# Branch A's attention values in plain fp32 passes, two heads as column tiles of one matmul group

## The chip, the cores and the metric

The kernel runs on one core of one Trainium2 chip. The metric is the device time of one launch in microseconds (us). Lower is better.

## The reference

One encoder layer is applied to two request groups ("prompt" and "sample", each 1024 tokens by 1024 channels) that share all weights. What matters of it:

```python
h = rms_norm(x, norm_g) * (1.0 + scale) + shift          # scale, shift, gate from silu(c) @ w_ada
qa, ka, va, za, qb, kb, vb, zb, ga, gb = split(h @ w_in)  # one input projection

# Branch A: 8 query heads, 2 key/value heads, head_dim 64, QK RMSNorm, axial rotary
p  = softmax(qa @ ka.T / 8)              # per query head; four query heads share one k and one v
oa = (p @ va) * silu(za)
# Branch B: 4 heads with two 64-dim softmax maps each, 128-dim values
ob = rms_norm((p0 - lam * p1) @ vb) * (1 - lam_init) * silu(zb)

merged = sigmoid(ga) * (oa @ w_proj_a) + sigmoid(gb) * (ob @ w_proj_b)
y = x + gate * (merged @ w_out)
```

All inputs and outputs are fp32.

## The kernel before, in words

The two groups are worked one after the other. In each, the kernel makes the normalised and modulated input `h`, projects it, runs the attention of Branch A (phases 0 and 1, four query heads each) and of Branch B (phases 2 to 5, one head each), then the gates, the two branch projections, their merge and the output projection.

**Precision.** Most matmuls multiply a high and a low part: an fp32 value is cut by ScalarE into an fp32r part (`hi`) and by VectorE into the remainder (`lo`), and hi·hi, hi·lo and lo·hi are added in PSUM, each product one fast fp32r pass. A matmul on operands that are viewed as plain fp32 needs no such split and is run by TensorE in several passes of its own; the profile shows it as two records.

**Units of attention.** `units_of` makes a list of units, `attention` steps through them. In Branch A a unit is one query head and a pair of 128-query tiles (`pr`), 32 units for each group. `scores` handles one tile per step: the scores by two matmul passes for each half of the 1024 keys (lines 834 and 835, into one of two score banks `s`), the row maximum on VectorE (836), its scaling (837) and the exponential (838) on ScalarE, which writes a probability buffer `p` of `ppool` (four of them). `swapped` gets the queries with their halves exchanged by four small DMAs per two heads (688, tile `sw`). One step later `flip` transposes the probabilities in 32x32 blocks on VectorE (871) and carries them by four DMAs (876) into the unit's transposed tile `q` of `qpool` (two of them), where the blocks land so that keys lie on partitions.

`a_values` then multiplies with v. `pT_pieces` cuts each quarter of the transposed probabilities into `hi` (ScalarE, 884) and `lo` (VectorE, 885, in place in `q`). The weights are v's tile of 128 keys, 64 columns of its high part beside 64 columns of its low part; the moving operand is 256 queries, once `hi` (896) and once `lo` (897), for eight key chunks: 16 matmuls. `PV_LAG` keeps the matmuls two pieces behind the cutting. At the end one half of the accumulator is copied by ScalarE (912), the other half added by VectorE (913), and 64 rows go out by DMA (917). The halves of v's tile are written in `kva_gen` (711 and 712). Branch B's `b_values` (936), by `WHOLE`, already takes v and probabilities as plain fp32, with 128-column weights.

**Order of work.** Beside the attention run "pieces" of other work that TensorE can do meanwhile: input projections (598, with the transposes 658), gate projections in `z_gen` (807, results through `zd` in DRAM), branch projections (1080) and the output projection (1111). `weave` takes steps from several generators in proportion to weights and with head starts that are written out as constants at the top (`Z_SHARE`, `ATT_W`, `IN_A`, `Z_A`, `LAST_ATT` and others; one row for each request group, one entry for each phase). Attention steps are issued with a raised priority (`AHEAD`), and a scheduler that simulates a timeline settles the order on each engine; the chip then runs each engine's queue in order.

**Column tiles** occur in two places: the adaLN matmuls of the first group (`ada`, reported at line 104, four tiles of 32 columns) and those of the gate (`gate_gen`, 530, four tiles of which two columns are used).

**The start.** The first group's input arrives in quarters of channels; squares, sum, inverse root (307 to 314), the spreading of the norm over partitions (`spread`, 321), then `ada` on the first weights, `ada_sum`, and the modulation.

Of the kernel before, what the change touches and what calls it, by code (L numbers as in the profile page):

```python
# [12 lines left out]
F32 = mybir.dt.float32  # L13
F32R = mybir.dt.float32r
# [6 lines left out]
P = 128  # L21
# [14 lines left out]

Z_SHARE = (
    (8, 21, 4, 2, 4, 3),
    (13, 12, 7, 3, 0, 6),
)  # L40
Z_HEAD = (8, 6)
Z_HEAD_A = (-0.3, -0.32)
ATT_W = (
    (0.944, 1.067, 1.232, 1.093, 1.03, 1.769),
    (1.017, 1.367, 1.063, 1.196, 0.764, 1.069),
)
IN_A = (
    (0.1, -0.07, 0.7, 0.05, 0.25, 0.15),
    (0.1, -0.05, 0.43, 0.3, 0.15, 0.55),
)  # L50
Z_A = (
    (0.25, 0.05, 0.2, -0.05, -0.1, 0.0),
    (0.03, 0.05, 0.35, 0.15, -0.3, -0.2),
)
LAST_ATT = (47, 43)
LAST_FILL = (22, 23)
GATED_A = (0.1, 0.1)
LATE_A = 1.0
QUARTER_P = 200
KV_STEPS = 12  # L60
GATE_AT = 9
FIRST_ATT = 15
FIRST_A = 0.16
TAIL = (2, 5)
TAIL_A = (1.15, 1.15)
LAG = 2
Z_FIRST = (9, 8)
Z_FIRST_A = (-0.05, 0.0)

CUTS = (3, 6)  # L70

BEHIND = 1.4
AHEAD = 100
PV_LAG = 2

WHOLE = (True, True)

# [30 lines left out]
def kernel(ctx: ExitStack, tc: tile.TileContext, t: dict):  # L108
# [4 lines left out]
    upool = ent(tc.tile_pool(name="upool", bufs=15))  # L113
    wpool = ent(tc.tile_pool(name="wpool", bufs=2))
    spool = ent(tc.tile_pool(name="spool", bufs=3))
    ppool = ent(tc.tile_pool(name="ppool", bufs=4))
    qpool = ent(tc.tile_pool(name="qpool", bufs=2))
    tpool = ent(tc.tile_pool(name="tpool", bufs=2))
    mpool = ent(tc.tile_pool(name="mpool", bufs=2))
# [19 lines left out]
    def gbank():  # L139
        turn[0] += 1  # L140
        if alone[0] and not early and turn[0] % 5 in (0, 2):
            return sbank()[:, :512]
        return fbank()
# [179 lines left out]
        nc.scalar.activation(rsb, bank, AF.Copy)  # L323
        return rsb

    def ada(wts, cpad):

        acc = gbank()
        for q, wt in enumerate(wts):
            for c in range(4):  # L330
                pe.matmul(
                    acc[32 * c : 32 * c + 32], cpad[:, q * 4 + c], wt[:, c], start=(q == 0), stop=(q == 1),
                    tile_position=(0, 32 * c),
                )
        part = rtile()
        act.activation(part, acc, AF.Copy)
        return part

    def ada_sum(part):
        ps = gbank()[:, :8].rearrange("p (t c g) -> p t c g", t=2, g=2)  # L340
# [55 lines left out]
    def start(ht):  # L396
        cpad = mtile("at", [P, 256], bufs=1).rearrange("p (c m) -> p c m", c=NCH)
        nc.vector.memset(cpad, 0.0)
        nc.scalar.activation(cT, ccol, AF.Tanh, scale=0.5)
        nc.vector.scalar_tensor_tensor(out=cT, in0=cT, scalar=1.0, in1=ccol, op0=ALU.add, op1=ALU.mult)  # L400
        nc.vector.tensor_scalar(out=cT, in0=cT, scalar1=0.5, scalar2=None, op0=ALU.mult)
        nc.vector.tensor_copy(cpad[:, :, :2], cT)
        xT = [load_xT0(0)]
        dma_next(bcol, t["b_col"])
        dma_next(gcol, t["g_col"])
        wts = [load_ada(n) for n in range(2)]
        kva_w.append(load_w(w_cols(w_in, (C_KA, 256)), early=True))
        kva_w.append(load_w(w_cols(w_in, (C_QA, 256)), early=True))
        wts += [load_ada(n) for n in range(2, 8)]

        rs = inv_rms(added(squares(xT[0])))
        nc.vector.tensor_scalar(out=bcol[:, 1, :], in0=bcol[:, 1, :], scalar1=1.0, scalar2=None, op0=ALU.add)
        rsb = spread(rs)
        early.update({n: four_sums() for n in range(2)})
        ps = ada_sum(ada(wts[:2], cpad))
        with tc.high_priority(offset=QUARTER_P):
            for quarter in range(4):
                cs = range(quarter * 2, quarter * 2 + 2)
                by_rms(xT[0], cs, rsb)
                split_early(kva_w[0][1], quarter)  # L420
                ada_end(quarter, ps)
                if quarter % 2 == 0:
                    add_h(ht, 0, quarter // 2)
                split_early(kva_w[1][1], quarter, act)
                modulated(ht, 0, xT[0], cs)
                split_early(kva_w[1][1], quarter, vec)
                for c in cs:
                    sums_early(ht, c, 0)
                part = ada(wts[quarter * 2 + 2 : quarter * 2 + 4], cpad) if quarter < 3 else None
                for c in cs:  # L430
                    sums_early(ht, c, 1)
                    if part is not None:
                        ps, part = ada_sum(part), None
        xT.append(load_xT0(1))
        kva_w.append((load_w(w_cols(w_in, (C_ZA, 256)), room=(utile(), utile())),))
        return lambda: inv_rms(added(squares(xT[1]))), lambda rs: start_late(ht, xT[1], rs)
# [226 lines left out]
    def pipelined(ht, w, front, back, given={}, rest=0):  # L663
# [14 lines left out]
            back(*pend.pop(0))  # L678
        yield 1

    def swapped(u):

        qs = u["q"]
        sw = mtile("sw", [P, 2, 256], F32R)[:, : len(qs)]
        sl = slice(u["pr"] * 256, u["pr"] * 256 + 256)
        for m, q in enumerate(qs):
            for a, b in ((LO, HI), (HI, LO)):
                dma(sw[a, m].bitcast(F32), q[b, sl].bitcast(F32))
        return sw
# [7 lines left out]
    def kva_gen(ht, out):  # L697
        w = kva_w[0][0] if early else load_w(w_cols(w_in, (C_KA, 256)))
        given = dict(enumerate(early.get(0, ())))
        k = v2(utile())  # L700
        va = utile().rearrange("p (n k d) -> p n k d", n=NTT, k=2)
        out["ka"], out["va"] = k, va

        def front(tt, ps):
            e = by_turns(tt)
            rs = tiny.tile([P, 4], F32, tag="rs", name=nm("rs"))[:, :2]
            x3, s3 = rows(ps[:, :128], 2, rs)
            e.tensor_tensor(out=x3, in0=x3, in1=rs.unsqueeze(2).to_broadcast([P, 2, HD]), op=ALU.mult)
            vp = ps[:, 128:256].rearrange("p (k d) -> p k d", k=2)
            vt = va[:, tt]  # L710
            nc.scalar.activation(vt[:, :, 0:64], vp, AF.Copy)
            nc.vector.tensor_tensor(out=vt[:, :, 64:128], in0=vp, in1=vt[:, :, 0:64].bitcast(F32), op=ALU.subtract)
            e.tensor_tensor(out=x3, in0=x3, in1=gka.unsqueeze(1).to_broadcast([P, 2, HD]), op=ALU.mult)
            rope(x3, s3, out["cosA"][:, tt : tt + 1], out["sinA"][:, tt : tt + 1], 16, e)
            return x3
# [126 lines left out]

    def scores(u, i):

        nm_ = len(u["q"])
        t, m = i // nm_, i % nm_
        qt = u["pr"] * 2 + t
        if "sw" not in u:
            u["sw"] = swapped(u)
        pt = ptile()  # L850
        su = u["su"][:, qt : qt + 1] if m == 0 else tiny.tile([P, 1], F32, tag="su", name=nm("su"))
        softmax_unit(u["q"][m][:, qt * P : (qt + 1) * P], u["rs"](qt, m), u["sw"][:, m, t * P : (t + 1) * P], u["k"][m], pt, su)
        if m == 0:
            u[t] = [pt]
        else:
# [3 lines left out]
                out=f, in0=f, scalar1=u["su"][:, qt : qt + 1], scalar2=nlam, op0=ALU.mult, op1=ALU.mult  # L859
            )  # L860
            u[t] += [pt, f]
        return t if m == nm_ - 1 else None

    def flip(u, t):

# [20 lines left out]
            yield cc, th, tl  # L886

    def a_values(u):
        acc = ps_a.tile([P, 512], F32, tag="a", name=nm("a"))[:, :256]
        ready = []  # L890

        def pv(cc, th, tl):
            for c in range(2):
                k = cc * 2 + c
                lt = u["v"](k)
                nc.tensor.matmul(acc, lt, th[:, c, :], start=(k == 0), stop=False)  # L896
                nc.tensor.matmul(acc, lt, tl[:, c, :], start=False, stop=(k == 7))  # L897

        for piece in pT_pieces(u):
            ready.append(piece)  # L900
            if len(ready) > PV_LAG:
                pv(*ready.pop(0))
            yield 1
        while len(ready) > 1:
            pv(*ready.pop(0))
            yield 1
        pv(*ready.pop())
        tmp = mtile("at", [P, 256], bufs=1)
        o = mtile("oo", [P, 256])
        j = u["j"]  # L910
        a, b = (slice(0, 64), slice(64, 128)) if j % 2 == 0 else (slice(64, 128), slice(0, 64))
        nc.scalar.activation(tmp[a], acc[b], AF.Copy)
        nc.vector.tensor_tensor(
            out=query_order(o[a]), in0=piece_order(acc[a]), in1=piece_order(tmp[a]), op=ALU.add
        )
        pr = u["pr"]
        dma(u["od"][pr // 2][a, (pr % 2) * 256 : (pr % 2 + 1) * 256], o[a])
        yield 1

    def b_values(u):  # L920
# [238 lines left out]

    def units_of(st):  # L1160

        def a_unit(half, i, pr):
            j = half * 4 + i
            kv = j // 4
            return {
                "q": [st["qa"][half][i % 2][:, i // 2]], "k": [st["ka"][:, kv]],
                "v": (lambda k: st["va"][:, k, kv, :]),
                "pr": pr, "j": j, "od": st["od"][j // 2], "su": st["suA"][:, j],
                "rs": lambda qt, m: st["rsA"][:, half, qt, i : i + 1],
            }  # L1170

        def b_unit(h, pr):
# [11 lines left out]
        units = []  # L1184
        for half in range(2):
            units += [
                (half, lambda a=(half, i, pr): a_unit(*a), lambda a=("qa", half, pr): there(*a))
                for i in (0, 2, 1, 3) for pr in range(4)
            ]
        for h in range(4):  # L1190
            units += [
# [136 lines left out]
```

## Time and profile before

| | us |
|---|---|
| median of 3 runs | 1944.08 |
| lowest and highest | 1943.26, 1944.20 |
| profiled execution, whole time | 1940.72 |
| profiled execution, span | 1938.9 |

In the rows of the profile PE is TensorE's matmuls, PEld its weight loads, DVE VectorE, ACT ScalarE, POOL GpSimd, SP the engine that issues the DMAs; L807 is line 807 of the kernel. A row of a group reads: line, engine, operation, output<-inputs, shapes, number, then busy us and mean ns of one, then the engine's idle time just before them and what ended it. A row of the waits reads: who waited for whom, us in total, times, longest. A row of the timeline reads: start, length, engine, line and operation, number of merged records, and idle time before it in brackets. Matmuls are pipelined, so the length of a record is longer than the distance to the next; what one costs is read from the starts. 64 units of Branch A, 32 of each group, lie between about 130 and 560 us and between about 1110 and 1500 us.

### The profile page before, as it was taken

To read this page: it belongs to the slowest core of one execution; us is meant where nothing else is said; L and a number is where in the kernel's file an instruction comes from. 1 tells how busy PE (TensorE), PEld (TensorE's weight loads), DVE (VectorE), ACT (ScalarE), POOL (GpSimd) and SP (SyncE) were. 2 spreads that over 40 slices of the span, in tenths; PEclk is the share of its full clock that TensorE was granted. 3 is DMA by queue.
4 is the path that set the end of the run, shared out by engine and by line. 5 is a ranking of instruction groups with operands and counts; after the bars stand their busy time and mean duration, and the time that the engine had idled before them with its cause. 6 is when DMAs were issued, how large, how long until landed. Compare 5 with 4: busy or idle time off the path is not lost.

```text
span 1938.9 us, 30718 instructions
## 1 busy us (share of the span) xinstructions
PE 1858.5 (96%) x10406; PEld 1606.0 (83%) x10406; DVE 1393.9 (72%) x2160; ACT 994.9 (51%) x2095; POOL 414.0 (21%) x766
## 2 busy tenths in 40 slices
PE   6899999999999999999999999999999999998999
PEld 4778888888878898777889888889878899777887
DVE  4768976777887667868465788777879777876731
ACT  3536766666765455424223566566767555552310
POOL 0342210022334241010124222002232323300000
PEclk9899999999999999999999999999999999999999
DMA  9125555655655435877641455655655443677632
GB/s 320 51 65 158 146 150 145 163 153 152 162 162 153 102 103 166 245 249 241 203 139 44 128 146 152 172 143 150 162 148 142 121 128 97 163 232 231 212 103 76
DMA packets 278140, 299.47 MB, mean 154 GB/s; under 512 B 38176, under 2 KB 228832, under 8 KB 277984
## 3 DMA queue, kind: packets, MB, share of 16 engines
q1 hardware_dynamic: 277984, 297.51, 54.6%
q8 instruction: 84, 1.38, 0.3%
q14 instruction: 72, 0.59, 0.1%
HBM read 137.91 MB, written 42.04 MB: 93 GB/s over the span
## 4 chain that ended last, share of the span: by engine, by line
PE 53%; DVE 16%; DMA 12%; ACT 6%; SPq 5%; issue 5%; POOL 2%; ACTq 0%; DVEq 0%; POOLq 0%
PE f L807 12%; PE f L598 12%; DMA q<-p 6%; PE f L1111 6%; PE f L1080 4%; DVE m L836 4%; SPq L876 4%; PE s L1111 3%; DVE p L871 3%; PE a L936 3%; PE s L834 3%; PE s L835 3%; DVE q L885 2%; ACT p L838 2%; PE s L1080 2%
## 5 line engine op out<-in xcount | busy, mean ns | idle before, releaser
L807 PE MATMUL f<-u,w 128*128 128x512 f32 x2184 | 560.0, 394 | 5.1 <-DVE w L203 1.8
L807 PEld LDWEIGHTS f<-u,w 128*128 128x128 f32 x2184 | 394.9, 188 | 81.5 <-DVE w L203 3.1
L598 PE MATMUL f<-w,u 128*128 128x256 f32 x3264 | 459.0, 286 | 3.3 <-DVE u L661 2.3
L598 PEld LDWEIGHTS f<-w,u 128*128 128x128 f32 x3264 | 432.1, 192 | 22.4 <-issue 2.0
L836 DVE TENSOR_REDUCE m<-s 128x1 f32<-128x1024 f32 x256 | 310.6, 1217 | 25.4 <-PE s L835 22.8
L871 DVE STREAM_TRANSPOSE p<-p 128x1024 f32<-128x1024 f32 x192 | 238.1, 1241 | 104.7 <-ACT p L838 100.8
L835 PE MATMUL s<-u,sw 128*128 128x512 f32 x512 | 203.9, 398 | 1.9 <-DMA sw<-u 1.9
L885 DVE TENSOR_TENSOR q<-q,hi 128x512 fp32r<-128x512 f32 x256 | 172.0, 691 | 37.9 <-ACT hi L884 36.6
L838 ACT ACTIVATE p<-s,m,rsA 128x1024 f32<-128x1024 f32 x128 | 153.9, 1202 | 72.1 <-DMA q<-p 70.1
L884 ACT ACTIVATE hi<-q 128x512 fp32r<-128x512 f32 x256 | 152.8, 623 | 73.8 <-DMA q<-p 37.1
L202 ACT ACTIVATE w<-st 128x512 fp32r<-128x512 f32 x188 | 109.6, 625 | 103.4 <-DMA st<-in_w_in_dram 39.5
L838 ACT ACTIVATE p<-s,m,rsB 128x1024 f32<-128x1024 f32 x128 | 154.3, 1206 | 13.9 <-DMA q<-p 7.4
L203 DVE TENSOR_TENSOR w<-st,w 128x512 fp32r<-128x512 f32 x188 | 126.0, 699 | 32.1 <-ACT w L202 31.4
L1080 PE MATMUL f<-u,w 128*128 128x512 f32 x576 | 139.1, 393 | 4.7 <-ACT u L1052 1.9
L896 PE MATMUL a<-hi,u 128*128 128x256 f32 x512 | 131.3, 283 | 2.2 <-ACT hi L884 1.0
L936 PE MATMUL a<-q,u 128*128 128x256 f32 x512 | 126.7, 388 | 5.4 <-DMA q<-p 2.5
L1080 PEld LDWEIGHTS f<-u,w 128*128 128x128 f32 x576 | 107.4, 188 | 29.3 <-ACT u L1052 2.3
L897 PE MATMUL a<-q,u 128*128 128x256 f32 x512 | 128.8, 285 | 1.6 <-DVE q L885 1.6
L752 POOL TENSOR_TENSOR row<-row,gB 128x96 f32<-128x96 f32 x64 | 28.7, 448 | 443.4 <-ACT row L619 443.3
L834 PE MATMUL s<-u 128*128 128x512 f32 x256 | 109.7, 429 | 10.2 <-ACT p L838 9.2
L936 PEld LDWEIGHTS a<-q,u 128*128 128x128 f32 x512 | 96.8, 195 | 21.2 <-issue 6.6
L835 PEld LDWEIGHTS s<-u,sw 128*128 128x128 f32 x512 | 97.5, 191 | 17.6 <-issue 2.0
(198 smaller groups left out, 2597.4 us busy)
## 6 DMA issues: line engine op xcount, KB each, us to landing
q<-p SPq DMA_DIRECT2D x768, 128.0 KB, 2.8
st<-in_w_in_dram SPq DMA_DIRECT2D x128, 256.0 KB, 3.2
zd<-ev SPq DMA_DIRECT2D x96, 256.0 KB, 2.5
sw<-u SPq DMA_DIRECT2D x256, 64.0 KB, 2.1
p<-zd SPq DMA_DIRECT2D x64, 256.0 KB, 4.4
u<-in_w_ada_dram SPq DMA_DIRECT2D x16, 512.0 KB, 8.8
st<-in_w_in_dram SPq DMA_DIRECT2D x64, 128.0 KB, 3.1
st<-in_w_out_dram SPq DMA_DIRECT2D x32, 256.0 KB, 3.8
```

Source lines behind the costliest of these rows:

```text
L598: nc.tensor.matmul(ps, lt[c][:, sl], w[c][:, wi, :], start=(k == 0), stop=(k == 23))
L807: nc.tensor.matmul(ps, w[c][:, wi, e * P : (e + 1) * P], rt[c], start=(k == 0), stop=(k == 23),)
L834: nc.tensor.matmul(s[:, sl], q, k[:, sl], start=True, stop=False)
L835: nc.tensor.matmul(s[:, sl], sw, k[:, sl], start=False, stop=True)
L836: nc.vector.tensor_reduce(out=m, in_=s, axis=AX.X, op=ALU.max, negate=True)
L838: nc.scalar.activation(pt.rearrange("p (j c a) -> p j c a", j=4, c=8), s.rearrange("p (c a j) -> p j c a", c=8, j=4), AF.Exp, scale=rs, bi ...
L871: nc.vector.transpose(pt, pt)
L884: nc.scalar.activation(th, tl.bitcast(F32), AF.Copy)
L885: nc.vector.tensor_tensor(out=tl, in0=tl.bitcast(F32), in1=th.bitcast(F32), op=ALU.subtract)
L936: nc.tensor.matmul(acc, u["v"][:, k], pT[:, k], start=(k == 0), stop=(k == 7))
L1080: nc.tensor.matmul(ps, w[:, c, wi, d * P : (d + 1) * P], o[:, oi, :], start=(k == 0), stop=(k == 11))
L1111: nc.tensor.matmul(ps, w[c][:, wi, e * P : (e + 1) * P], m[:, mi, :], start=(k == 0), stop=(k == 23))
```

## The change

- **Units.** A unit of Branch A becomes two query heads of the same key/value head and one tile of 128 queries, again 32 units for each group. Its two score steps are the two heads. The tile order becomes four query tiles for the one pair of heads, the same four for the other pair, then the other four tiles.
- **Values.** v is kept as plain fp32, 64 columns a key/value head, by one ScalarE copy. `a_values` waits one step (`A_WAIT`), then issues the matmuls of all eight key chunks in one step: for each chunk and each of the two heads one plain fp32 matmul with 64-column weights and 128 moving columns, the first head into partitions 0 to 63 of the accumulator and the second into 64 to 127. The probabilities are not split. One ScalarE copy empties the accumulator; every second unit sends 128 rows by 256 queries out in one DMA.
- **Swapped queries** are fetched on even query tiles for two tiles at once and used again on the odd one.
- **Buffers.** `ppool` has five probability buffers instead of four.
- **The start.** `ada` is cut in two halves; the first stands ahead of `spread` in the program, the second with its copy behind it.
- **Pieces.** The constants that share out and offset the pieces are set anew.

```diff
-    (13, 12, 7, 3, 0, 6),
+    (13, 12, 5, 3, 2, 6),
 )
-Z_HEAD = (8, 6)
+Z_HEAD = (7, 6)
...
 ATT_W = (
-    (0.944, 1.067, 1.232, 1.093, 1.03, 1.769),
-    (1.017, 1.367, 1.063, 1.196, 0.764, 1.069),
+    (0.825, 1.067, 1.07, 1.093, 1.03, 1.769),
+    (0.938, 1.664, 1.177, 1.271, 0.764, 1.144),
 )
 IN_A = (
-    (0.1, -0.07, 0.7, 0.05, 0.25, 0.15),
-    (0.1, -0.05, 0.43, 0.3, 0.15, 0.55),
+    (0.3, -0.07, 0.7, 0.05, 0.25, 0.15),
+    (0.1, -0.05, 0.33, 0.3, -0.03, 0.55),
 )
...
+A_WAIT = 1
+A_CUTS = ()
...
-    ppool = ent(tc.tile_pool(name="ppool", bufs=4))
+    ppool = ent(tc.tile_pool(name="ppool", bufs=5))
...
+    def ada_half(wt, cpad, q, acc=None):
+
+        acc = acc or gbank()
+        for c in range(4):
+            pe.matmul(
+                acc[32 * c : 32 * c + 32], cpad[:, q * 4 + c], wt[:, c], start=(q == 0), stop=(q == 1),
+                tile_position=(0, 32 * c),
+            )
+        return acc
...
-        rs = inv_rms(added(squares(xT[0])))
+        sq = squares(xT[0])
+        rs = inv_rms(added(sq))
+        first = ada_half(wts[0], cpad, 0)
...
         rsb = spread(rs)
+        part = ada_part(ada_half(wts[1], cpad, 1, first))
         early.update({n: four_sums() for n in range(2)})
-        ps = ada_sum(ada(wts[:2], cpad))
+        ps = ada_sum(part)
...
+        if u.get("qt", 0) % 2:
+            return turned["sw"]
         qs = u["q"]
-        sw = mtile("sw", [P, 2, 256], F32R)[:, : len(qs)]
+        sw = turned["sw"] = mtile("sw", [P, 2, 256], F32R)
...
-        va = utile().rearrange("p (n k d) -> p n k d", n=NTT, k=2)
+        va = utile().bitcast(F32)[:, :1024].rearrange("p (n k d) -> p n k d", n=NTT, k=2)
...
-            vt = va[:, tt]
-            nc.scalar.activation(vt[:, :, 0:64], vp, AF.Copy)
-            nc.vector.tensor_tensor(out=vt[:, :, 64:128], in0=vp, in1=vt[:, :, 0:64].bitcast(F32), op=ALU.subtract)
+            nc.scalar.activation(va[:, tt], vp, AF.Copy)
...
     def a_values(u):
-        acc = ps_a.tile([P, 512], F32, tag="a", name=nm("a"))[:, :256]
...
-        tmp = mtile("at", [P, 256], bufs=1)
-        o = mtile("oo", [P, 256])
...
-        nc.scalar.activation(tmp[a], acc[b], AF.Copy)
-        nc.vector.tensor_tensor(
-            out=query_order(o[a]), in0=piece_order(acc[a]), in1=piece_order(tmp[a]), op=ALU.add
-        )
+        acc = ps_a.tile([P, 512], F32, tag="a", name=nm("a"))[:, :P]
+        pT = u["pT"].bitcast(F32).rearrange("p (i t c b) -> p t c i b", i=4, t=2, c=8)
+        for _ in range(A_WAIT):
+            yield 1
+        for k in range(NCH):
+            for e in range(2):
+                nc.tensor.matmul(acc[e * 64 : e * 64 + 64], u["v"](k), pT[:, e, k], start=(k == 0), stop=(k == 7))
+            if k in A_CUTS:
+                yield 1
+        t = u["qt"] % 2
+        if t == 0:
+            turned["o"] = mtile("oo", [P, 256])
+        o = turned["o"]
+        nc.scalar.activation(o[:, t * P : (t + 1) * P], acc, AF.Copy)
         pr = u["pr"]
-        dma(u["od"][pr // 2][a, (pr % 2) * 256 : (pr % 2 + 1) * 256], o[a])
+        if t:
+            dma(u["od"][pr // 2][:, (pr % 2) * 256 : (pr % 2 + 1) * 256], o)
         yield 1
...
-                for i in (0, 2, 1, 3) for pr in range(4)
+                for quarter in ((0, 4), (4, 8)) for i in range(2) for qt in range(*quarter)
```

More of the change, by code (lines that the diff above doesn't have):

```diff
@@ L38 @@
     (8, 21, 4, 2, 4, 3),
-    (13, 12, 7, 3, 0, 6),
+    (13, 12, 5, 3, 2, 6),
 )
-Z_HEAD = (8, 6)
+Z_HEAD = (7, 6)
 Z_HEAD_A = (-0.3, -0.32)
 ATT_W = (
-    (0.944, 1.067, 1.232, 1.093, 1.03, 1.769),
-    (1.017, 1.367, 1.063, 1.196, 0.764, 1.069),
+    (0.825, 1.067, 1.07, 1.093, 1.03, 1.769),
+    (0.938, 1.664, 1.177, 1.271, 0.764, 1.144),
 )
 IN_A = (
-    (0.1, -0.07, 0.7, 0.05, 0.25, 0.15),
-    (0.1, -0.05, 0.43, 0.3, 0.15, 0.55),
+    (0.3, -0.07, 0.7, 0.05, 0.25, 0.15),
+    (0.1, -0.05, 0.33, 0.3, -0.03, 0.55),
 )
 Z_A = (
-    (0.25, 0.05, 0.2, -0.05, -0.1, 0.0),
-    (0.03, 0.05, 0.35, 0.15, -0.3, -0.2),
+    (0.25, 0.05, 0.1, -0.05, -0.1, -0.05),
+    (0.03, 0.07, 0.25, 0.15, -0.3, -0.1),
 )
-LAST_ATT = (47, 43)
+LAST_ATT = (47, 41)
 LAST_FILL = (22, 23)
-GATED_A = (0.1, 0.1)
-LATE_A = 1.0
+GATED_A = (0.1, -0.15)
+LATE_A = 0.95
 QUARTER_P = 200
@@ L64 @@
 TAIL = (2, 5)
-TAIL_A = (1.15, 1.15)
+TAIL_A = (1.15, 1.2)
 LAG = 2
 Z_FIRST = (9, 8)
-Z_FIRST_A = (-0.05, 0.0)
+Z_FIRST_A = (-0.05, -0.05)
 CUTS = (3, 6)
@@ L324, in spread, with ada_part @@
         return rsb
[L326 to L333, printed above, removed]
-                )
+    def ada_half(wt, cpad, q, acc=None):
[6 more added lines that the diff above has]
+        return acc
+    def ada_part(acc):
         part = rtile()
@@ L337, in ada @@
         return part
+    def ada(wts, cpad):
+        return ada_part(ada_half(wts[1], cpad, 1, ada_half(wts[0], cpad, 0)))
     def ada_sum(part):
@@ L679, in pipelined @@
         yield 1
+    turned = {}
     def swapped(u):
+        if u.get("qt", 0) % 2:
+            return turned["sw"]
         qs = u["q"]
-        sw = mtile("sw", [P, 2, 256], F32R)[:, : len(qs)]
+        sw = turned["sw"] = mtile("sw", [P, 2, 256], F32R)
         sl = slice(u["pr"] * 256, u["pr"] * 256 + 256)
@@ L843, in scores @@
     def scores(u, i):
-        nm_ = len(u["q"])
-        t, m = i // nm_, i % nm_
-        qt = u["pr"] * 2 + t
         if "sw" not in u:
@@ L850, in scores @@
         pt = ptile()
+        if "j" in u:
+            qt = u["qt"]
+            t = qt % 2
+            softmax_unit(
+                u["q"][i][:, qt * P : (qt + 1) * P], u["rs"](qt, i), u["sw"][:, i, t * P : (t + 1) * P], u["k"],
+                pt, u["su"][:, i, qt : qt + 1],
+            )
+            u[i] = [pt]
+            return i
+        t, m = i // 2, i % 2
+        qt = u["pr"] * 2 + t
         su = u["su"][:, qt : qt + 1] if m == 0 else tiny.tile([P, 1], F32, tag="su", name=nm("su"))
@@ L861, in scores @@
             u[t] += [pt, f]
-        return t if m == nm_ - 1 else None
+        return t if m else None
     def flip(u, t):
@@ L888, in a_values @@
     def a_values(u):
-        acc = ps_a.tile([P, 512], F32, tag="a", name=nm("a"))[:, :256]
[L890 to L902, printed above, removed]
-            yield 1
[L904 to L907, printed above, removed]
-        tmp = mtile("at", [P, 256], bufs=1)
-        o = mtile("oo", [P, 256])
[L910 to L913, printed above, removed]
-            out=query_order(o[a]), in0=piece_order(acc[a]), in1=piece_order(tmp[a]), op=ALU.add
-        )
+        acc = ps_a.tile([P, 512], F32, tag="a", name=nm("a"))[:, :P]
+        pT = u["pT"].bitcast(F32).rearrange("p (i t c b) -> p t c i b", i=4, t=2, c=8)
+        for _ in range(A_WAIT):
+            yield 1
+        for k in range(NCH):
[8 more added lines that the diff above has]
+        nc.scalar.activation(o[:, t * P : (t + 1) * P], acc, AF.Copy)
         pr = u["pr"]
-        dma(u["od"][pr // 2][a, (pr % 2) * 256 : (pr % 2 + 1) * 256], o[a])
+        if t:
+            dma(u["od"][pr // 2][:, (pr % 2) * 256 : (pr % 2 + 1) * 256], o)
         yield 1
@@ L1160, in units_of, with a_unit @@
     def units_of(st):
-        def a_unit(half, i, pr):
-            j = half * 4 + i
-            kv = j // 4
+        def a_unit(half, i, qt):
+            j = half * 4 + i * 2
             return {
[L1166 to L1169, printed above, removed]
+                "q": [st["qa"][half][e][:, i] for e in range(2)], "k": st["ka"][:, half],
+                "v": (lambda k: st["va"][:, k, half]),
+                "qt": qt, "pr": qt // 2, "j": j, "od": st["od"][j // 2], "su": st["suA"][:, j : j + 2],
+                "rs": lambda qt, e: st["rsA"][:, half, qt, 2 * i + e : 2 * i + e + 1],
             }
@@ L1186, in units_of @@
             units += [
-                (half, lambda a=(half, i, pr): a_unit(*a), lambda a=("qa", half, pr): there(*a))
-                for i in (0, 2, 1, 3) for pr in range(4)
+                (half, lambda a=(half, i, qt): a_unit(*a), lambda a=("qa", half, qt // 2): there(*a))
+                for quarter in ((0, 4), (4, 8)) for i in range(2) for qt in range(*quarter)
             ]
```

## Prediction

> **What bounds the kernel now.** I read the page first, then busy times by stretch (the attention of the two request groups lies at about 160 to 790 us and 1090 to 1790 us, Branch A in the first 400 us of each), then the waits, then TensorE's timeline around single groups of matmuls.
>
> ```profile
> span 1938.9 us, 30718 instructions
> ...
> PE 1858.5 (96%) x10406; PEld 1606.0 (83%) x10406; DVE 1393.9 (72%) x2160; ACT 994.9 (51%) x2095; POOL 414.0 (21%) x766
> ```
> ```profile
> 160.00:565.00 405.00, 397.81 (x2355) 350.44 (x2354) 321.82 (x451) 262.76 (x546) 84.73 (x156) 1.00 0.59 155
> 1090.00:1500.00 410.00, 399.42 (x2349) 350.60 (x2348) 328.19 (x456) 266.17 (x554) 84.28 (x156) 1.00 0.58 151
> ```
> The second fence has the stretch, its length, then the busy time of PE, PEld, DVE, ACT, POOL, then granted clock, DMA share and GB/s. TensorE bounds the kernel, and Branch A most of all: 7.2 and 10.6 us idle, 17.8 together. VectorE (79 and 80%) and ScalarE (65%) have room on average, but what little TensorE loses there it loses to them:
>
> ```profile
> PE s L834 <- ACT p L838: 14.9, 14, 2.7
> ...
> PE a L936 <- DMA q<-p: 2.5, 2, 1.3
> ```
> ```profile
> ACT p L838 <- DMA q<-p: 77.6, 48, 4.1
> ...
> PEld s L834 <- ACT p L838: 22.5, 23, 2.8
> ```
> The scores of L834 wait until the exponential of L838 has emptied a score bank, and that exponential waits 48 times until a probability buffer has been carried off. So two numbers decide: what Branch A's value matmuls cost TensorE, and how much of the 17.8 us comes back.
>
> **TensorE's price of the value matmuls.** Before, a unit is one head by 256 queries: eight key chunks by two passes (high and low part, L896 and L897), 16 matmuls, 64 units in all. After, a unit is two heads by 128 queries: eight chunks by two heads, plain fp32, weights of 64 columns, 128 columns moving, the heads in the two halves of the array.
>
> ```profile
> 319.75 0.28 PE L896 MATMUL a<-hi,u 128*128 128x256 f32 x1
> ...
> 321.17 0.86 PE L807 MATMUL f<-u,w 128*128 128x512 f32 x3
> ...
> 575.46 3.69 PE L936 MATMUL a<-q,u 128*128 128x256 f32 x16 [0.83 <-DMA sw<-u]
> 579.08 1.03 PE L530 MATMUL f<-wg,cT 128*2 128x256 f32 x12
> ```
> Twelve of the present passes (the six pairs between the first two rows) take 1.42 us, 0.118 each: 16 x 0.118 = 1.89 us a unit. Branch B's values are plain fp32 already: eight matmuls of a unit give 16 records, so one plain matmul is two records, and here 16 take 3.62 us, 0.226 each with the switch behind them. A record of 256 columns thus costs about two passes.
>
> Whether two heads really run side by side, the two places with column tiles tell:
>
> ```profile
> 40.31 1.12 PE L104 MATMUL s<-w,u 128*128 128x256 f32 x8
> 41.36 1.92 PE L104 MATMUL f<-u,at 128*32 128x512 f32 x16
> 43.22 0.98 PE L104 MATMUL s<-w,u 128*128 128x256 f32 x6
> ```
> ```profile
> 672.53 1.04 PE L530 MATMUL f<-wg,cT 128*2 128x256 f32 x16
> 673.50 0.50 PE L834 MATMUL s<-u 128*128 128x512 f32 x1
> 673.84 0.39 PE L835 MATMUL s<-u,sw 128*128 128x512 f32 x1
> 674.07 0.39 PE L834 MATMUL s<-u 128*128 128x512 f32 x1
> ```
> Both are plain fp32 in four column tiles. L530: 16 records in 0.97 us, where 16 records of the same width took 3.62 above: four at a time. The adaLN matmuls: 16 records of twice the width in 1.86 us. With four records deep per tile, 8s + e = 1.86 and 4s + e = 0.97 give s = 0.222 per 256-column record and e = 0.08 for leaving the mode. A 128-column record is half, 0.111. Entering: the eight matmuls before 41.36 take 1.05 where 8 x 0.118 is 0.95, 0.10 more; after leaving, the second matmul starts after 0.34 instead of 0.23, 0.11 more. A switch there and back is 0.29. Two tiles with 16 records each: 16 x 0.111 + 0.29 = 2.07 us, if the unit's 32 records stand in one group. They are issued in one step, with no cut between them. So +0.18 a unit, **+11 us** in 64. From below: transposes of 128 columns, each with a load of its own, run
>
> ```profile
> 951.67 0.60 PE L562 MATMUL f<-ident,rsx 128*128 128x128 f32 x4
> 952.10 0.60 PE L562 MATMUL s<-ident,rsx 128*128 128x128 f32 x4
> 952.46 2.33 PE L1111 MATMUL f<-u,w 128*128 128x512 f32 x9
> ```
> eight in 0.79 us, 0.099; with that and no switch a unit is 1.58, -20 us in all. From above: no two at a time, 32 x 0.111 + 0.29 = 3.84, +125 us. I take +11, since tiles and switch are both seen on this chip; only the width of 64 is not.
>
> **ScalarE, VectorE, and what comes back.**
>
> ```profile
> L885 DVE TENSOR_TENSOR q<-q,hi 128x512 fp32r<-128x512 f32 x256 | 172.0, 691 | 37.9 <-ACT hi L884 36.6
> ...
> L884 ACT ACTIVATE hi<-q 128x512 fp32r<-128x512 f32 x256 | 152.8, 623 | 73.8 <-DMA q<-p 37.1
> ```
> ```profile
> L913 DVE TENSOR_TENSOR oo<-a,at 64x256 f32<-64x256 f32 x64 | 26.8, 419 | 2.2 <-ACT at L912 1.1
> ...
> L912 ACT ACTIVATE at<-a 64x256 f32<-64x256 f32 x64 | 24.2, 378 | 3.7 <-PE a L897 2.3
> ...
> L712 DVE TENSOR_TENSOR u<-f,u 128x128 fp32r<-128x128 f32 x12 | 3.5, 291 | 7.6 <-ACT u L711 7.3
> ...
> L711 ACT ACTIVATE u<-f 128x128 fp32r<-128x128 f32 x12 | 3.3, 272 | 0.0
> ```
> The splits of the probabilities go whole (153 us of ScalarE, 172 of VectorE), the sum of the two halves too (27 of VectorE), v's remainder (some 4.6 for 16 tiles). One ScalarE copy of 128x128 takes the place of L912; by L711's 0.272 that is 17 us instead of 24. In the 815 us of Branch A ScalarE falls from 529 to about 370, VectorE from 650 to about 450. None of it is on the path by itself. It pays where TensorE waits: the late exponentials, and the waits of L896 and L897 on their pieces, which cease to exist. The fifth probability buffer acts on the same place: 77.6 us of ScalarE's waiting for a buffer, and behind that ScalarE's queue and the score banks. Both bounds are rows: nothing comes back, or all 17.8 (small gaps that the modelled ends hide are left out). I take **-15**, nearer the top, because the releasers named are the engines that are relieved.
>
> The added wait is that the whole group now stands on TensorE's queue until eight transfers have landed, with all fillers behind it. Branch B does that already, and its price is the row of L936 above: 2.5 us in 32 units; as the steps lie a unit behind the flip here too, I count about 2, within the 2.8 us that the 15 leaves. The transfers are otherwise equal: eight for the transposed probabilities a unit, four for the swapped queries every second unit instead of two each; SyncE's output issues halve from 64 to 32.
>
> **The start.** Half of the first adaLN group moves ahead of the spreading of the norm.
>
> ```profile
> 12.75 1.87 PE L307 MATMUL f<-ones_c,q 128*128 128x1 f32 x8 [12.75 <-DVE q L299]
> ...
> 16.27 1.12 PE L321 MATMUL s<-ident,rs 128*128 128x128 f32 x4 [1.65 <-POOL rs L314]
> ...
> 17.31 3.64 PE L104 MATMUL f<-u,at 128*32 128x512 f32 x16
> ...
> 21.02 0.60 ACT L104 ACTIVATE row<-f 128x512 f32<-128x512 f32 x1 [3.00 <-PE f L104]
> ```
> TensorE stands idle 1.65 us while the inverse root is made, and half of the 3.64 us fits there; ScalarE waits 3.0 us for the end of the group. If the weights have landed by 14.6 us the chain shortens by 1.8 us, if not by less; **-1.8**, from 0 to -2.
>
> **Pieces set anew.** A few filler pieces of the second request group move from Branch B's phases, and shares and offsets change. What they can touch is the idle time of these stretches (columns as above):
>
> ```profile
> 565.00:700.00 135.00, 129.36 (x858) 114.03 (x856) 99.27 (x158) 72.87 (x158) 45.67 (x97) 0.97 0.48 129
> ...
> 800.00:900.00 100.00, 90.63 (x401) 73.63 (x402) 75.79 (x117) 32.70 (x61) 6.13 (x8) 1.00 0.82 252
> ...
> 1700.00:1790.00 90.00, 82.93 (x363) 67.38 (x362) 63.77 (x89) 34.21 (x67) 8.15 (x12) 0.98 0.76 232
> ```
> 22 us idle in these three. No row prices an order of issue; it can give or take up to 10. I take **-3**, a seventh of it: a Branch A that needs less of the two side engines leaves less work pending at its end.
>
> **The sum.** +11 - 15 - 1.8 - 3 = -8.8 against the profiled execution's 1940.7 (its span of 1938.9 and 1.8 around it). The median of the runs is 1944.1, 3.4 above, so 1944.1 - 8.8 = 1935.3.
>
> **The rivals.**
> - The groups are broken up by fillers. Branch B's plain groups are sometimes broken by filler matmuls, which there need no change of mode:
>
> ```profile
> 663.18 0.60 PE L936 MATMUL a<-q,u 128*128 128x256 f32 x2
> 663.43 0.47 PE L598 MATMUL f<-w,u 128*128 128x256 f32 x1
> ```
> In Branch A each break adds 0.29, 18.6 us in 64 units. At two groups a unit the sum is +30 - 10 (half of the groups then wait longer) - 1.8 = +18, 1962. Slower; it decides from about 1.5 groups a unit. For it: the scheduler mixes. Against: the groups of L530 and of adaLN stand whole above. Chance 0.17.
> - TensorE pays, and the idle time does not return, because scores, exponential and transpose form a chain that one buffer does not shorten: +11 - 3 - 1.8 = +6, 1950. Chance 0.11.
> - Weight loads bound the tiles. The nearest load row is plain fp32:
>
> ```profile
> L658 PEld LDWEIGHTS f<-ident,row 128*128 128x128 f32 x184 | 24.6, 142 | 9.5 <-POOL row L647 2.3 <-issue 0.8
> ```
> At 0.142 a record instead of 0.111 a unit is 2.56, +43 in all, 1944 + 43 - 20 = 1967. Against it: L562's 0.099 with loads of 128 columns. The Trainium skill, page "TensorE: Matmul & The Clock Gate", section "Back-to-back issue gap", gives about 81 ns for a sustained 128-column matmul with its load; by that, an estimate, two passes are 0.162 and the time near 1988. The 0.099 here speaks against it. Chance 0.05.
> - Two tiles do not run side by side at 64 columns: +125 - 18 - 1.8 - 3 = +102, 2046. Against it are the four tiles above. Chance 0.05.
> - The switch hides and everything returns: -20 to 0 for TensorE, -17.8, -1.8, -3: at -8 for TensorE 1913. Chance 0.10.
>
> The Trainium skill, "TensorEngine Tiling (Array Packing)", section "Tiling Modes", says that a change of mode drains the engine; the 0.29 above is that drain, and the first rival is its rule carried further.
>
> **The numbers.** The likeliest case, with the remaining 0.52, gives 1935, its own range 1923 to 1945. The range for all reaches from 1914 to 1962: the high end is two groups a unit, the low end the last rival. About 0.2% (3.9 us) is what a measurement can tell from no change. Faster by more than that 0.60 (the best case, 0.49 of the likeliest and a hundredth of the first rival), within it 0.09 (0.03 of the likeliest, 0.06 of the second rival), slower 0.31 (the rest).
>
> **What would show it.** Right: records of 64 columns, 32 in one run, some 2.0 to 2.1 us from the first to the next other matmul; no L884 or L885 in Branch A; idle TensorE under 5 us in both Branch A stretches; the adaLN row copied at about 19.2 us instead of 21.0. Wrong: runs of 2 to 8 records, or a unit over 2.2 us; TensorE waiting at the group for the transposed probabilities; or idle time that returns in Branch B's stretches.

## The result and the profile after

The changed kernel takes 2004.47 us (median of 4 runs, 2004.36 to 2007.75) against 1943.67 for the kernel before on the same chip: ratio 1.0326, 95% interval 1.0298 to 1.0355. It is 61 us slower, where 1935 was forecast, and lies outside the range of 1914 to 1962.

The page of the changed kernel, its first lines and two groups (L915 is the value matmul of Branch A; L608, L819, L846 and L847 are the former L598, L807, L834 and L835):

```profile
span 2002.7 us, 32130 instructions
...
PE 1951.8 (97%) x11430; PEld 1606.1 (80%) x11430; DVE 1213.9 (61%) x1824; ACT 853.1 (43%) x1839; POOL 400.7 (20%) x766
...
L915 PE MATMUL a<-q,u 128*64 128x128 f32 x2048 | 195.4, 281 | 0.0
L915 PEld LDWEIGHTS a<-q,u 128*64 128x64 f32 x2048 | 129.8, 136 | 66.7 <-issue 49.4
```

Its first Branch A stretch by windows, columns as in the prediction:

```profile
160.00:565.00 405.00, 405.00 (x2456) 302.02 (x2455) 193.28 (x226) 157.28 (x340) 50.59 (x96) 1.00 0.52 136
```

VectorE's busy time fell by 180 us and ScalarE's by 142; the prediction's rows of the splits and copies add up to some 202 and 160. TensorE, idle for 7.2 us of this stretch before, is never idle now. So the idle time did come back; but TensorE has 93 us more busy time in all. The waits say where to look (the first row is from the kernel before, the others from the changed one):

```profile
DVE m L836 <- PE s L835: 22.8, 28, 2.7
```
```profile
DVE m L848 <- PE s L847: 225.3, 109, 10.4
```
```profile
PEld a L915 <- issue: 49.4, 172, 0.4
PEld f L819 <- issue: 14.7, 86, 0.2
PEld f L608 <- issue: 14.6, 85, 0.2
```

The row maximum waited 22.8 us for TensorE before and waits 225.3 now (L848 is the former L836): VectorE has to wait for TensorE. In the three rows on "issue", weight loads (those of the value matmuls and those of the fillers) are late although they wait for nothing that the profile shows: the loads of the value matmuls 172 times, 0.29 us on average. That looks like a lost overlap of loads with matmuls, and TensorE's timeline shows where:

```profile
302.18 0.39 PE L846 MATMUL s<-u,u 128*128 128x512 f32 x1
302.50 0.65 PE L915 MATMUL a<-q,u 128*64 128x128 f32 x6
303.08 0.50 PE L846 MATMUL s<-u,u 128*128 128x512 f32 x1
303.42 0.40 PE L847 MATMUL s<-u,sw 128*128 128x512 f32 x1
...
304.22 0.43 PE L915 MATMUL a<-q,u 128*64 128x128 f32 x2
304.58 0.50 PE L847 MATMUL s<-u,sw 128*128 128x512 f32 x1
305.01 1.53 PE L915 MATMUL a<-q,u 128*64 128x128 f32 x24
306.47 1.20 PE L819 MATMUL f<-u,w 128*128 128x512 f32 x4
...
312.66 0.44 PE L915 MATMUL a<-q,u 128*64 128x128 f32 x4
313.03 0.50 PE L846 MATMUL s<-u,u 128*128 128x512 f32 x1
...
320.36 1.97 PE L915 MATMUL a<-q,u 128*64 128x128 f32 x32
322.25 0.50 PE L847 MATMUL s<-u,sw 128*128 128x512 f32 x1
322.59 0.40 PE L846 MATMUL s<-u,u 128*128 128x512 f32 x1
```

The unit at 320.36 stands in one group: 32 records, 16 matmuls, in 1.89 us, 0.118 a matmul, the same 1.89 that the prediction read for the split values before. The one at 302.50 stands in three pieces of 3, 1 and 12 matmuls with scores between. Its three matmuls take 0.58 us, its lone one 0.36; the two at 312.66 take 0.37, hardly more than one. In TensorE's order of instructions the 64 units stand in 272 runs; 182 of these are a single matmul, and only 6 units are whole. What cuts in: gate projections (92 runs begin behind one), input projections (84), scores (81) and transposes (15). A run is here a stretch of value matmuls with no other matmul between them.

### The profile page after: what moved, and what is told of

Its sections match the earlier page's. It is cut to its first block, busy times and chain, and to the rows that moved or that the text cites. A ratio compares the mean times of both kernels' runs of the same rounds, so it can differ in the third digit from the quotient of the medians.

```text
span 2002.7 us, 32130 instructions
## 1 busy us (share of the span) xinstructions
PE 1951.8 (97%) x11430; PEld 1606.1 (80%) x11430; DVE 1213.9 (61%) x1824; ACT 853.1 (43%) x1839; POOL 400.7 (20%) x766
## 4 chain that ended last, share of the span: by engine, by line
PE 84%; DMA 6%; DVE 5%; ACT 2%; issue 1%; POOL 1%; SPq 1%; DVEq 0%; ACTq 0%; POOLq 0%
PE f L819 24%; PE f L608 19%; PE a L915 9%; PE s L846 6%; PE f L1119 5%; PE s L847 5%; PE a L944 4%; PE s L1119 3%; PE f L1088 3%; PE s L1088 2%; PE s L106 1%; DMA row<-zd 1%; PE f L668 1%; DVE m L848 1%; DVE p L890 1%
## 5 line engine op out<-in xcount | busy, mean ns | idle before, releaser
L819 PE MATMUL f<-u,w 128*128 128x512 f32 x2184 | 577.2, 398 | 2.2 <-ACT ev L801 1.5
L608 PE MATMUL f<-w,u 128*128 128x256 f32 x3264 | 478.5, 288 | 4.2 <-DVE u L106 1.7
L819 PEld LDWEIGHTS f<-u,w 128*128 128x128 f32 x2184 | 397.5, 188 | 92.5 <-issue 14.7
L608 PEld LDWEIGHTS f<-w,u 128*128 128x128 f32 x3264 | 434.2, 191 | 37.4 <-issue 14.6
L848 DVE TENSOR_REDUCE m<-s 128x1 f32<-128x1024 f32 x256 | 310.7, 1218 | 227.3 <-PE s L847 225.3
L847 PE MATMUL s<-u,sw 128*128 128x512 f32 x512 | 206.3, 404 | 0.0
L915 PE MATMUL a<-q,u 128*64 128x128 f32 x2048 | 195.4, 281 | 0.0
L915 PEld LDWEIGHTS a<-q,u 128*64 128x64 f32 x2048 | 129.8, 136 | 66.7 <-issue 49.4
L1088 PE MATMUL f<-u,w 128*128 128x512 f32 x576 | 141.4, 395 | 5.1 <-ACT u L1060 3.0
L944 PE MATMUL a<-q,u 128*128 128x256 f32 x512 | 126.0, 381 | 3.0 <-DMA q<-p 1.6
L671 DVE TENSOR_TENSOR u<-f,u 64x256 fp32r<-64x256 f32 (+1 forms) x208 | 84.1, 406 | 61.3 <-ACT u L670 55.8
L846 PE MATMUL s<-u 128*128 128x512 f32 x256 | 110.8, 433 | 4.2 <-ACT p L850 4.1
L847 PEld LDWEIGHTS s<-u,sw 128*128 128x128 f32 x512 | 97.0, 190 | 20.0 <-issue 5.0
L1119 PE MATMUL f<-u,w 128*128 128x512 f32 x480 | 111.2, 389 | 0.0
L628 ACT ACTIVATE row<-f 128x256 f32<-128x256 f32 (+1 forms) x104 | 38.5, 370 | 167.0 <-PE f L608 162.7
```

The lines of the kernel that those rows point to most:

```text
L608: nc.tensor.matmul(ps, lt[c][:, sl], w[c][:, wi, :], start=(k == 0), stop=(k == 23))
L819: nc.tensor.matmul(ps, w[c][:, wi, e * P : (e + 1) * P], rt[c], start=(k == 0), stop=(k == 23),)
L846: nc.tensor.matmul(s[:, sl], q, k[:, sl], start=True, stop=False)
L847: nc.tensor.matmul(s[:, sl], sw, k[:, sl], start=False, stop=True)
L848: nc.vector.tensor_reduce(out=m, in_=s, axis=AX.X, op=ALU.max, negate=True)
L915: nc.tensor.matmul(acc[e * 64 : e * 64 + 64], u["v"](k), pT[:, e, k], start=(k == 0), stop=(k == 7))
```

## The experiments

The main theory is "breaks": the loss is the number of runs times the price of a break, 208 more than 64. From the rows above, a lone matmul costs 0.36 where it would cost 0.118 in a group, 0.24 more; entering the mode costs 0.10 and the second matmul after it 0.11 (0.34 instead of 0.23 at 322.25): 0.45 in all. Its rivals are that plain fp32 passes are dear in themselves, and that the newly set pieces bring the loss. Each ratio below compares with the kernel before on the same chip, where that took 1937 to 1944 us, so a difference between runs on two chips can be off by a few us.

**Whole groups.** Pin and raise the value matmuls, so that the program has 64 runs:

```diff
-        for k in range(NCH):
-            for e in range(2):
-                nc.tensor.matmul(acc[...], u["v"](k), pT[:, e, k], start=(k == 0), stop=(k == 7))
-            if k in A_CUTS:
-                yield 1
+        with tc.high_priority(offset=600):
+            for k in range(NCH):
+                for e in (1, 0):
+                    mm = nc.tensor.matmul if k == 0 and e else pe.matmul
+                    mm(acc[...], u["v"](k), pT[:, e, k], start=(k == 0), stop=(k == 7))
```

> The changed kernel, with the 16 value matmuls of each Branch A unit kept together on TensorE's queue (the later head first, the other 15 pinned behind it, a raised priority): the groups stand in 64 runs instead of 272. Theory 'breaks': each break of a group costs 0.4 to 0.47 us (a lone matmul takes 0.36 us and two changes of mode about 0.2), so 208 fewer give 1907 us if TensorE stays full, and up to 1940 if the idle time of before comes back. Rival 'plain passes': the plain fp32 passes themselves are dearer, whatever their order; then the time stays over 1985. Rival 'pieces': the newly set pieces bring the loss; then over 1985 too.

Measured: 1914.65 us (1911.3 to 1915.85), ratio to before 0.987, interval 0.9832 to 0.9908. That is 90 us less than the changed kernel, and 23 less than the kernel before. Both rivals fall as the main cause: plain passes and new pieces are still there, and the loss is gone. TensorE's idle time is the same in both kernels (50.9 us), so the whole difference of their profiled spans, 89.3 us, is TensorE's busy time. Its page, its two Branch A stretches by windows, and one unit on TensorE's timeline:

```profile
span 1913.4 us, 32086 instructions
...
PE 1862.5 (97%) x11430; PEld 1592.1 (83%) x11430; DVE 1212.5 (63%) x1824; ACT 852.2 (45%) x1839; POOL 402.7 (21%) x766
```
```profile
160.00:490.00 330.00, 330.00 (x2405) 281.65 (x2399) 189.02 (x221) 153.19 (x332) 47.88 (x90) 1.00 0.61 161
1095.00:1365.00 270.00, 270.00 (x2059) 229.37 (x2059) 175.17 (x189) 137.87 (x294) 29.16 (x48) 1.00 0.70 183
```
```profile
302.93 1.24 PE L608 MATMUL f<-w,u 128*128 128x256 f32 x9
304.01 0.40 PE L819 MATMUL f<-u,w 128*128 128x512 f32 x1
304.24 1.24 PE L608 MATMUL f<-w,u 128*128 128x256 f32 x9
305.41 0.32 PE L917 MATMUL a<-q,u 128*64 128x128 f32 x1
305.42 0.32 PE L106 MATMUL a<-q,u 128*64 128x128 f32 x1
305.57 0.27 PE L917 MATMUL a<-q,u 128*64 128x128 f32 x1
305.58 1.80 PE L106 MATMUL a<-q,u 128*64 128x128 f32 x29
307.31 0.50 PE L846 MATMUL s<-u,u 128*128 128x512 f32 x1
307.64 0.39 PE L847 MATMUL s<-u,sw 128*128 128x512 f32 x1
```

A unit takes 1.90 us; nine L608 before it last 1.17 where nine others at 302.93 last 1.08 (entering, about 0.10), and the second matmul after it starts after 0.33 (0.10 more). That is 2.10 a unit; the prediction had 2.07. The wait of the value loads on "issue" fell with the number of runs:

```profile
PEld a L917 <- issue: 10.5, 31, 0.4
```

Against before, TensorE's busy time is 4.0 us longer (1862.5 to 1858.5) and its idle time 29.5 shorter (50.9 to 80.4): the 25.5 of the span. Of the 29.5, the 17.8 of Branch A's stretches are all there (these are shorter now, 330 and 270 us, with more of the fillers behind them); the other 12 lie outside Branch A, some 4 each before, between and after its two stretches. By the lines, 2.10 against 1.89 would be 13 us more busy time in 64 units, and it rose by 4.0. A part of that gap is the 1.89: counted from start to start over the whole trace, the split passes of before took 125.5 us, 1.96 a unit. Where the rest was saved is open.

**226 runs.** As above without the raised priority:

```diff
-        with tc.high_priority(offset=600):
+        with tc.high_priority(offset=0):
```

> As the kernel with whole groups, but without the raised priority: the later head first and the matmuls of a unit pinned behind each other, with fillers still let in between. 226 runs instead of 272. Theory 'breaks': 46 x 0.47 = 22 us less than the changed kernel, about 1983 (1980 to 1990). Rivals 'plain passes' and 'pieces': 2000 to 2006.

Measured: 1984.49 us (1983.63 to 1986.43), ratio 1.0236 (1.0204 to 1.0268). Putting the later head first and pinning the others saves 46 runs, the priority 162.

**359 runs.** More breaks in the changed kernel:

```diff
-A_CUTS = ()
+A_CUTS = (1, 3, 5)
```

> The changed kernel with three cuts in each unit's value matmuls (after chunks 1, 3 and 5): 359 runs instead of 272. Theory 'breaks': 87 x 0.4 to 0.47 more, 2039 to 2045. Rivals 'plain passes' and 'pieces': no change beyond 5 us, 2000 to 2010.

Measured: 2042.52 us (2040.44 to 2046.32), ratio 1.0536 (1.0501 to 1.057). The four points lie on a line: from 64 runs (1914.65) to 272 (2004.47) 0.432 us a run, from 226 to 272 0.434, from 272 to 359 0.437. Three of the points come from one chip, and these alone give 0.431 (64 to 226) and 0.436 (226 to 359).

**The change with the old pieces.** The constants as before; the program then has 415 runs:

> The changed kernel with the constants of the pieces as before the change. Its value matmuls then stand in 415 runs instead of 272. Theory 'breaks': 0.435 us a run, so 143 x 0.435 = 62 more than the changed kernel and 5 for the old pieces as measured with whole groups: about 2072 (2055 to 2080). Rival 'the new pieces cost time in themselves' (28 us with the split values): 1976 to 2004.

Measured: 2073.35 us (2072.7 to 2074.64), ratio 1.0698 (1.0677 to 1.072). With the same constants and whole groups (below) it is 1920.11: 351 runs cost 153.2 us, 0.437 a run. So the new pieces do help the changed kernel by 69 us, all but some 6 of it through the order that they happen to give the matmuls.

**Whole groups with the old pieces.** The same constants in the kernel with 64 runs:

> The kernel with whole groups (64 runs) with the constants of the pieces as before the change. If the newly set pieces bring something with the new values, it is slower than the kernel with whole groups (1915) by 3 to 20 us; if the returned idle time of TensorE alone makes its gain, it lies within 3 us of it.

Measured: 1920.11 us (1918.2 to 1921.21), ratio 0.9898 (0.9876 to 0.9921). The new pieces are worth 5.5 us there.

**Pieces alone.** The kernel before with the new constants:

> The kernel before with only the constants of the pieces set as in the change; Branch A's values still split in high and low parts. The prediction's step: -3 against before, between -10 and +10. Rival 'pieces are the loss': over +40. Theory 'breaks': no part of the 60 us is here.

Measured: 1965.99 us (1964.45 to 1967.46), ratio 1.0139 (1.0111 to 1.0167): +28, outside my -10 to +10 and short of the rival's +40. The same constants cost 28 us with split values and give 5.5 with plain ones. Its profiled span is 23.8 us longer than before, and its windows show where more than half of that goes: TensorE is idle for 15.6 and 16.0 us in Branch A's stretches instead of 7.2 and 10.6.

```profile
160.00:565.00 405.00, 389.45 (x2291) 342.70 (x2290) 307.37 (x432) 250.99 (x525) 82.96 (x154) 0.99 0.56 146
...
1090.00:1500.00 410.00, 394.03 (x2316) 346.77 (x2314) 319.29 (x446) 258.38 (x541) 82.83 (x152) 0.99 0.57 148
```

**Four buffers.** Whole groups with `ppool` at four:

```diff
-    ppool = ent(tc.tile_pool(name="ppool", bufs=5))
+    ppool = ent(tc.tile_pool(name="ppool", bufs=4))
```

> The kernel with whole groups with four probability buffers instead of five. Theory of the prediction (ScalarE's waits for a buffer reach TensorE through the score banks): 2 to 10 us slower than 1915. Rival (with the splits gone ScalarE has slack and the fifth buffer is idle): within 2 us of it.

Measured: 1915.39 us (1913.56 to 1920.92), ratio 0.988 (0.9853 to 0.9907). The fifth buffer is worth nothing here that these runs can tell.

**The start alone.** The kernel before with only the adaLN group cut in two:

> The kernel before with only the first adaLN group cut in two halves, one ahead of the spreading of the norm. The prediction's step: 1.8 us less than before, 1942 (1940 to 1944). Rival: the weights land late or the later part of the start sets the time; no change.

Measured: 1940.56 us (1937.11 to 1945.13) against 1938.15, ratio 1.0009 (0.9993 to 1.0025). The row is copied at 18.71 us instead of 21.02, and the last early products start at 54.73 instead of 58.18:

```profile
18.71 0.60 ACT L104 ACTIVATE row<-s 128x512 f32<-128x512 f32 x1 [0.86 <-PE s L104]
```
```profile
54.73 0.50 PE L104 MATMUL s<-w,u 128*128 128x256 f32 x2 [1.18 <-ACT u L104]
```

So the lead of 3.4 us is real at 55 us and is gone at the end. Between 60 and 160 us TensorE was busy 89.7 us there, 91.2 before, at a mean granted clock of 0.90 and 0.92 (0.93 and 1.00 in the 60 us ahead of that); whether that is all of it is open.

**One head after the other.** Whole groups, but all chunks of one head ahead of the other's:

```diff
-            for k in range(NCH):
-                for e in (1, 0):
+            for e in (1, 0):
+                for k in range(NCH):
```

> The kernel with whole groups, but in each group all eight chunks of one head first, then all eight of the other, so that the two halves of the array have no work at the same time. If the heads do run side by side in the change, 16 x 0.108 = 1.7 us more in each of 64 units: 1915 + 110 = 2025. If the order within a group is of no account (the hardware overlaps them anyway, or never does), 1915.

Measured: 1998.78 us (1997.25 to 2001.56), ratio 1.0307 (1.0282 to 1.0331): 84 more than with the heads in turn, 1.31 a unit. A group takes 3.25 us instead of 1.90:

```profile
306.96 0.43 PE L917 MATMUL a<-q,u 128*64 128x128 f32 x2
307.23 3.06 PE L106 MATMUL a<-q,u 128*64 128x128 f32 x30
310.21 0.73 PE L846 MATMUL s<-u,u 128*128 128x512 f32 x2
```

The heads do run side by side in the change, as long as they come in turn: the group takes 1.71 times as long without. The expected 110 was too much. The starts of the single records in the trace lie 0.109 us apart, as expected, but around the change of heads two such series run beside each other, four records of each, which saves some 0.4 us a unit. Why the next head starts ahead there is open.

**Two units in a group.** The matmuls of an even query tile wait for those of the odd one and go out with them, 33 runs and one copy for both. The steps of the values also come sooner behind the transposes (`A_BEHIND`, 0.6 of a unit instead of 1.4):

```diff
+A_BEHIND = 0.6
...
+        if u["qt"] % 2 == 0:
+            turned["even"] = u
+            return
+        both = (u, turned["even"])
...
-            steps += [(n + BEHIND + i / nv, ph, n, i, False) for i in range(nv)]
+            steps += [(n + (A_BEHIND if ph < 2 else BEHIND) + i / nv, ph, n, i, False) for i in range(nv)]
```

> As the kernel with whole groups, but the value matmuls of an even query tile wait for those of the odd one, and both units' 32 stand in one group with one copy out: 33 runs instead of 64. Theory 'breaks' (here only the change of mode and the copy, about 0.3 us a run): 10 us less than 1915, 1905. Rival: the transposed probabilities of the even tile hold their buffer longer, so the next transposes and their transfers start late and TensorE waits; 1915 to 1935.

Measured: 1902.45 us (1901.55 to 1902.88), ratio 0.9815 (0.9792 to 0.9838), 12 less than with whole groups: the fastest version, 35 us under the kernel before. A group of 64 records takes 3.65 us:

```profile
316.69 0.32 PE L924 MATMUL a<-q,u 128*64 128x128 f32 x1
316.70 0.32 PE L107 MATMUL a<-q,u 128*64 128x128 f32 x1
316.86 0.27 PE L924 MATMUL a<-q,u 128*64 128x128 f32 x1
316.86 3.55 PE L107 MATMUL a<-q,u 128*64 128x128 f32 x61
320.34 0.50 PE L847 MATMUL s<-u,u 128*128 128x512 f32 x1
```

The rival of the held buffers falls. What part the moved steps have in the 12 us was not tried; the runs alone explain about 11 (below).

## Why the prediction was wrong

- **The step that failed** is the term "+11 us" for the value matmuls, in its condition "if the unit's 32 records stand in one group" with the reason "They are issued in one step, with no cut between them". The order of writing does not set the order on the queue: the scheduler let fillers and scores in, 4.25 runs a unit instead of one. By the profiled spans the change is +4.0 us of TensorE's busy time with whole groups, +89.3 for the breaks and -29.5 of idle time, 63.8 in all.
- **What spoke against breaks was misread.** The prediction held against this rival that "the groups of L530 and of adaLN stand whole above". The adaLN matmuls are issued by `pe.matmul`, which keeps them in program order, as the value matmuls of the change are not. And of the four groups of L530 two are broken in the same trace, one of them right where the prediction quotes it, with twelve of its 16 records:

```profile
579.08 1.03 PE L530 MATMUL f<-wg,cT 128*2 128x256 f32 x12
580.04 0.50 PE L834 MATMUL s<-u 128*128 128x512 f32 x1
...
581.17 0.60 PE L530 MATMUL f<-wg,cT 128*2 128x256 f32 x4
```

Branch B's 32 plain groups, of which the prediction showed one broken (663.18), stand in 78 runs there; only 18 are whole.

- **The first rival was the right mechanism**, with a chance of 0.17, and was mis-sized twice. It took two groups a unit; there are 4.25. It took 0.29 a break, the change of mode alone; the line through the points gives 0.435. The starts of the single records show the rest. A record of the one head and one of the other start together, and the next pair 0.109 us later; but the first step of a run takes 0.16, and from its last pair to the next other matmul it is 0.20. So each run costs 0.15 more than its pairs, where the prediction had 0.08. And a matmul without a neighbour leaves the other half of the array empty: a run of one takes as long as a run of two, one of three as long as one of four (0.58 and 0.59). Of the 272 runs 230 have an odd number of matmuls. Summed over the trace, the runs take 176.4 us instead of 121.6 with whole groups, 55 more: 31 for 208 further ends, 24 for the missing neighbours. The rest of the 89.3, some 34 us or 0.17 a break, is about what the lines show for the change of mode, 0.2 going in and coming out together. In the kernel with two units in a group nearly all runs are even: 31 runs fewer at 0.15 and 0.2 are 11 us, 12 were measured.
- **The Trainium skill's rule** ("TensorEngine Tiling (Array Packing)", section "Tiling Modes", that a change of mode drains the engine) agrees with the traces: 0.10 going in, and the second matmul coming out 0.10 to 0.11 late. That the lost time is a drain is the page's word; no trace shows it. The Trainium skill's 81 ns for a sustained 128-column matmul with its load ("TensorE: Matmul & The Clock Gate", section "Back-to-back issue gap") does not fit: a record of 128 columns, two passes by the prediction's count, starts 0.109 after the one before it, with its load, when one tile runs alone.
- **Right:** tiles of 64 columns run side by side (84 us more with one head after the other); a whole unit costs 2.10 us, 2.07 was forecast; the idle 17.8 us of Branch A all come back, 15 was taken; the signs named for being wrong came, runs of 2 to 8 records above all; the group's wait for the transposed probabilities comes to 0.7 us in two places, where about 2 were counted.
- **Right in size for a wrong reason:** of the sides of ScalarE that were counted, the fifth buffer gives nothing; with four the time is 0.7 us apart. The new units and values bring the idle time back without it; which part of them does was not tried.
- **Mis-sized even with whole groups:** there the kernel is 23.5 us faster than before, where the prediction had 8.8. TensorE's term measured +4.0 instead of +11, and 29.5 us of idle time came back where -15, -1.8 and -3 were taken.
- **Pieces:** -3 taken; -5.5 with whole groups. In the change itself they are worth -69, through the breaks, a way in which the prediction did not look for them.
- **The start:** -1.8 taken; the row comes 2.3 us earlier alone and 2.6 in the change, and nothing of it is left at the end.

## What to carry to other kernels

In this kernel column tiles that alternate with full-array matmuls were paid by the number of runs, not of matmuls alone: count the runs in the engine's order before trusting the price of a matmul, give each run an even share of both halves, and keep a group together by pinning its members behind the one whose data comes last and raising its priority. That the source writes a group in one piece does not keep it in one piece on the queue, and a group that stands whole in one place may have been pinned there, or be one of several that do not. When a change makes its mechanism work and the time still rises, look for waits on "issue" in front of the loads: here they stood at 49.4 us with 272 runs and at 10.5 with 64.

## What the runs showed of the hardware

A lone plain fp32 matmul with 64-column weights takes 0.36 us between full-array matmuls, two of them in the two halves 0.37, and 16 that alternate between the halves 1.90, 0.118 each. The records of one 64-column tile start 0.109 us apart, whether the other tile works beside it or not. A run of column tiles between full-array matmuls costs 0.15 us beyond its pairs of records and about 0.2 on the matmuls around it, and 0.11 more if a matmul has no neighbour: 0.435 us a run in this kernel on a full TensorE, from 64 to 415 runs.
